# Where the seven-product pairs stand: w_out and gate/up shifted by one pair, and `down` begun with plain steps

## The chip, the cores and the metric

One NeuronCore of a Trainium2 chip runs the kernel. Its engines each work through an instruction queue of their own, in program order, and wait for each other by semaphores: TensorE (PE in the profile, with its weight loads as PEld), VectorE (DVE), ScalarE (ACT), GpSimd (POOL, hardly used here) and SyncE (SP, which issues the DMAs). Matmul results go to PSUM, everything else lies in SBUF. The metric is the device time of one execution in microseconds, the median of several runs.

## What is computed

A decoder block on 256 tokens of width 2048: RMSNorm, two attention branches merged through sigmoid gates, an output projection with a residual, RMSNorm, a SwiGLU feed-forward of width 5632 with a residual, and a last RMSNorm. The change touches what follows the two branches:

```python
mixed = g_a * (y_a @ w_branch_a[l]) + g_b * (y_b @ w_branch_b[l])
h = h + mixed @ w_out[l]                                   # 2048 x 2048
hn = rmsnorm(h, ffn_norm[l])
h = h + (jax.nn.silu(hn @ w_gate[l]) * (hn @ w_up[l])) @ w_down[l]
return rmsnorm(h, final_norm)
```

All inputs and the output are float32.

## The kernel before

**Precision.** [...] A product is made of three matmuls: hi x hi, lo x hi, hi x lo. For weights, ScalarE writes `wh` (L927) and VectorE `wl` (L928).

**Jobs and steps.** The program is a list of jobs. A plain job multiplies one slab of 512 output columns: the 256 tokens are two row tiles t = 0, 1, and each has one PSUM accumulator of 128x512. The reduction goes in groups of four k-tiles (one DMA of 1 MB into a `raw` buffer) and each group in two steps of two k-tiles. So a plain step has 2 x 2 x 3 = 12 matmuls of 512 columns (L1026 for hi x hi and lo x hi, L1031 for hi x lo).

**Pairs with seven products.** Gate and up, and the slabs of `down` two by two, are taken as pairs: slabs a and b share the left operand. With the chunks of 512 along the reduction numbered 0, 1, 2, ..., chunks 0 and 1 of both slabs make a 2 x 2 block product (two token tiles by two chunks, two chunks by two slabs), which is done with seven products instead of eight, P1 to P7. Four accumulators are named by row tile and slab: 11, 21 (slab a) and 12, 22 (slab b). The products need sums of the left operand's blocks (`row_sums`, made once for a left operand by four VectorE adds and a cut) and differences of weights: four subtractions T1 to T4 of VectorE (L843, 128x2048), done in place in the raw buffers. A step of a product has 6 matmuls. The other chunks are plain, in steps written `a20` here: slab a, chunk 2, first k-tile 0. Four results that are needed alone are copied out of PSUM by ScalarE (`alone`, L683).

**Order.** The steps form one list. At step s the program first issues the weight cuts of step s + 3 (`split_until(s + AHEAD)`, with four buffers each for `wh` and `wl`), then whatever was put off to this step by `later` or `at`, then the matmuls of s. Each engine then executes in that order. The weights have 6 raw buffers by this part of the program; a buffer's next load is issued when its last cut has been issued. Everything of 128x1024 elements (left operands, their cuts, sums, results) lies in a pool of 33 slots. PSUM has four banks for accumulators and four for transposes.

**Around the change.** The four w_out slabs wo0 to wo3 are plain jobs with two accumulators each. After each, `wout_done` adds the residual (L643), sums the squares (ScalarE, L166), scales the rows by an estimate of the norm from the first slab (`hr`, L654; its root and `invert`, L155 to L159), and transposes them (`turned`, L207; PE, then ScalarE to `hF`). `cut` makes hi and lo of the transposed chunk (L217, L218). The true norm enters later as `hs`. Then follow the pairs gu0 to gu10 of gate and up, and dn0 and dn1 of `down`; each gate/up pair gives one chunk `aF` of the left operand of `down`. `feed` cuts such a chunk shortly before `down` uses it; `leave` adds the residual to the results of dn0 and multiplies by the last norm's gain. The products stand at the start of every pair, with chunk 2 and 3's steps for slab a between them:

P1, a20, P5, P2, a22, P3, P6, a30, P4, P7, a32, b20, b22, b30, b32, then all other chunks.

Of the kernel before, what the change touches and what calls it, by code (L numbers as in the profile page):

```python
# [24 lines left out]
F32R = mybir.dt.float32r  # L25
# [4 lines left out]
P = 128  # L30
NT = 2
# [37 lines left out]
def block_kernel(ctx: ExitStack, tc, x, positions, attn_norm, w_in, q_norm, w_uq, kv_norm, w_ukv,  # L69
# [72 lines left out]
    L = {}  # L142


    def rstd(ss, n, name):

        v, r, t = [const([P, NT], name + x) for x in ("_v", "", "_t")]

        def root():
            nc.vector.tensor_reduce(out=v, in_=ss, axis=mybir.AxisListType.X, op=OP.add)  # L150
            nc.vector.tensor_scalar(v, v, 1.0 / n, EPS, op0=OP.mult, op1=OP.add)
            nc.scalar.activation(t, v, AF.Sqrt)
# [167 lines left out]
    def pair(w, kt, ops, begin, name):  # L320
        jobs.append(dict(w=w, kt=kt, ops=ops, begin=begin, name=name))

    later_q = {}
    now = [0]
# [291 lines left out]
                nc.vector.tensor_mul(g[:, t], ps[t], g[:, t])  # L616
        return done

    mh, ml = [], []
    hop, hF, aF, aop = {}, {}, {}, {}  # L620
    ssh = const([P, NT, 4], "ssh")
    ssf = const([P, NT, 4], "ssf")
    R["h"], h_root, h_invert = rstd(ssh, D, "rstd_h")
    R["h0"], h0_root, h0_invert = rstd(ssh[:, :, 0:1], 512, "rstd_h0")
    hs = const([P, NT], "hs")

    def wa_done(c):
        def done(ps):
            a, b = gates["a", c], gates["b", c]
            for t in range(NT):  # L630
                nc.vector.tensor_mul(a[:, t], ps[t], a[:, t])
            nc.vector.tensor_add(b, a, b)
            mh.append(big([P, 4, S], f"mh{c}", F32R))
            ml.append(big([P, 4, S], f"ml{c}", F32R))
            spread(2, b, mh[c], ml[c], f"mT{c}")
        return done

    def wout_done(c):

        def done(ps):  # L640
            h = xt[c]
            for t in range(NT):
                nc.vector.tensor_add(h[:, t], ps[t], h[:, t])  # L643
                sumsq(h[:, t], ssh[:, t, c:c + 1])
            d = 4 if c == 0 else 1
            if c == 0:
                later(1, h0_root)
                later(3, h0_invert)
            st = {}

            def rows():
                st["n"] = big([P, NT, 512], f"hr{c}")
                for t in range(NT):
                    nc.scalar.mul(st["n"][:, t], h[:, t], R["h0"][:, t:t + 1])  # L654
                hF[c] = big([P, 4, S], f"hF{c}")

            def ready():
                hop[c] = cut(hF[c], f"h{c}")
                if c == 1:
                    hop["s"], add, finish = row_sums(hF[0], hF[1], "h")  # L660
                    later(1, add)
                    later(2, finish)
            later(d, rows)
            for i in range(2):
                later(d + 1 + i, lambda i=i: turned(st["n"], hF[c], f"hT{c}", 2 * i, "ffn", 4 * c))
            later(d + 3, ready)
            if c == 3:
                later(3, h_root)
                later(5, h_invert)

                def both():
                    v = L["h0_v"]
                    nc.vector.tensor_mul(hs, v, R["h0"])
                    nc.vector.tensor_mul(hs, hs, R["h"])
                later(6, both)
        return done

    def alone(jb, A, B):

# [2 lines left out]
        for u, dst, key in (("P1", A[:, 0], "22"), ("P5", B[:, 1], "12"), ("P6", B[:, 0], "22"), ("P7", A[:, 1], "22")):  # L682
            later(pos[u], lambda dst=dst, key=key: nc.scalar.copy(dst, ps[key]))  # L683

    def gu_begin(c):
        def begin(jb):
            ps, pos = jb["accs"], jb["pos"]
            A, B = big([P, NT, 512], f"ga{c}"), big([P, NT, 512], f"up{c}")
            alone(jb, A, B)

            def gate():
                for t, k in enumerate(("11", "21")):
                    nc.vector.tensor_add(A[:, t], ps[k], A[:, t])
# [24 lines left out]
    def dn_begin(j):  # L718
        def begin(jb):
            ps, pos = jb["accs"], jb["pos"]  # L720
            A, B = big([P, NT, 512], f"dA{j}"), big([P, NT, 512], f"dB{j}")
            alone(jb, A, B)
            for i, x in enumerate((A, B)):
                later(pos["P7"] + 3 + i, lambda i=i, x=x: nc.vector.tensor_add(xt[2 * j + i], xt[2 * j + i], x))
# [75 lines left out]
        gate_job("a", c)  # L800
    for c in range(4):
        job(w_branch_a[:, 512 * c:512 * (c + 1)], 8, ylhs("a"), wa_done(c), f"wa{c}")
    for c in range(4):
        job(w_out[:, 512 * c:512 * (c + 1)], 16, lhs_of(mh, ml), wout_done(c), f"wo{c}")
    for c in range(11):
        pair((w_gate[:, 512 * c:512 * (c + 1)], w_up[:, 512 * c:512 * (c + 1)]), 16, hop, gu_begin(c), f"gu{c}")
    for j in range(2):
        pair([w_down[:, 512 * c:512 * (c + 1)] for c in (2 * j, 2 * j + 1)], 44, aop, dn_begin(j), f"dn{j}")


    groups, steps = [], []
# [20 lines left out]
    def pair_steps(jb):  # L832


        ops, n = jb["ops"], jb["kt"] // 4
        wa, wb = jb["w"]
        G = {}

        def get(*cs):
            for x, c in cs:  # L840
                G[x, c] = add_group((wa, wb)[x], 4 * c, 4)

        sub = lambda o, x, y: (lambda: nc.vector.tensor_sub(raws[G[o]], raws[G[x]], raws[G[y]]))  # L843
        get((0, 0), (1, 0), (0, 2), (0, 1), (1, 1), (0, 3), (1, 2), (1, 3), *[(x, c) for c in range(4, n) for x in range(2)])

        def seven(name, key, src, lhs, pre=None):
            for k0 in (0, 2):
                add_step(jb, G[src], k0, [(key, lhs(k0))], pre if k0 == 0 else None, name)
# [7 lines left out]
        seven("P1", "22", (0, 0), A(0, 0), sub((1, 0), (1, 0), (0, 0)))  # L856
        eight(0, 2, 0)
        seven("P5", "12", (1, 0), S_(1))
        seven("P2", "11", (0, 1), A(1, 0), sub((1, 0), (1, 1), (1, 0)))
        eight(0, 2, 2)  # L860
        seven("P3", "12", (1, 1), S_(4), sub((0, 0), (1, 0), (0, 0)))
        seven("P6", "22", (1, 0), S_(2), sub((0, 1), (0, 1), (1, 0)))
        eight(0, 3, 0)
        seven("P4", "21", (0, 1), A(1, 1))
        seven("P7", "22", (0, 0), S_(3))
        eight(0, 3, 2, "a")
        for c in (2, 3):
            for k0 in (0, 2):
                eight(1, c, k0, "b")
        for c in range(4, n):  # L870
# [132 lines left out]
    for s, st in enumerate(steps):  # L1003
# [64 lines left out]
```

## Time and profile before

| what | value |
|---|---|
| median of 3 runs (lowest, highest) | 1347.22 us (1346.87, 1348.03) |
| profiled execution, its own time | 1348.63 us |
| span of its instructions | 1346.8 us |
| PE busy, DVE busy, ACT busy | 1305.4, 993.2, 782.8 us |
| mean granted TensorE clock | 0.943 |

The span runs from the first to the last instruction of the program; the execution's own time is 1.8 us more. A busy PE is one with a matmul in it. Idle time of an engine matters where another engine that sets the end has to wait for it. [...]

### The profile page before, as it was taken

What the parts mean: (1) busy time and instruction counts of PE and PEld (TensorE: products, weight loads), DVE (VectorE), ACT (ScalarE), POOL (GpSimd) and SP (SyncE); (2) the same over time, 40 slices, a digit from 0 to 9 for tenths busy, and PEclk for the clock granted to TensorE, in tenths of its full rate; (3) what the DMA queues carried; (4) which work ended last, traced back from release to release, by engine and by line L of the source; (5) the groups of instructions that cost most, each with busy time, mean ns of one, the idle gap of its engine ahead of it and who ended that gap; (6) DMA issues with size and microseconds to landing.
All of it is one profiled execution on the core that took longest, in us unless ns stands there. A gap on an engine that the chain in (4) does not pass through costs nothing.

```text
span 1346.8 us, 15873 instructions
## 1 busy us (share of the span) xinstructions
PE 1305.4 (97%) x5990; PEld 1081.8 (80%) x5990; DVE 993.2 (74%) x1212; ACT 782.8 (58%) x1000; POOL 2.1 (0%) x11
## 2 busy tenths in 40 slices
PE   8999999999999999998999999999999989998997
PEld 6888888888888888776887878778787868886885
DVE  5766667674565565578888998889888997579654
ACT  6455555654444454656666666667666665446553
POOL 0000000000000000000000000000000000000000
PEclk9999999999999999999999999999999989998998
DMA  8565544455555565543557545674457637553731
GB/s 295 187 205 182 164 159 153 160 174 189 187 183 160 190 244 188 188 157 118 173 209 250 191 151 185 223 249 156 159 186 249 220 124 250 190 185 108 267 125 63
DMA packets 126969, 249.06 MB, mean 185 GB/s; under 512 B 4486, under 2 KB 9132, under 8 KB 126892
## 3 DMA queue, kind: packets, MB, share of 16 engines
q1 hardware_dynamic: 126620, 247.78, 54.8%
q8 instruction: 47, 0.77, 0.2%
q10 hardware_dynamic: 272, 0.26, 0.1%
q14 instruction: 30, 0.25, 0.1%
HBM read 245.93 MB, written 2.10 MB: 184 GB/s over the span
## 4 chain that ended last, share of the span: by engine, by line
PE 92%; DVE 5%; ACT 2%; issue 1%; DMA 0%; ACTq 0%; SPq 0%; DVEq 0%
PE acc L1026 58%; PE acc L1031 29%; DVE wl L928 2%; DVE raw L843 1%; PE aT_tp L207 1%; ACT wh L927 1%; PE sb L435 1%; ACT junk L166 1%; PE ya L471 0%; PE yb L471 0%; DMA x<-in_x_dram 0%; PE sa L435 0%; PE hT_tp L207 0%; PE xT_tp L183 0%; ACT hr L654 0%
## 5 line engine op out<-in xcount | busy, mean ns | idle before, releaser
L928 DVE TENSOR_TENSOR wl<-raw,wh 128x1024 fp32r<-128x1024 f32 (+2 forms) x546 | 649.2, 1211 | 289.7 <-ACT wh L927 265.8
L927 ACT CAST wh<-raw 128x1024 fp32r<-128x1024 f32 (+2 forms) x546 | 568.1, 1044 | 406.0 <-PE acc L1026 359.6
L1026 PE MATMUL acc<-wh,xh 128*128 128x512 f32 (+1 forms) x512 | 139.4, 394 | 0.0
L1026 PE MATMUL acc<-wh,xl 128*128 128x512 f32 (+1 forms) x512 | 135.5, 387 | 0.0
L1031 PE MATMUL acc<-wl,xh 128*128 128x512 f32 (+1 forms) x512 | 135.3, 386 | 0.0
L843 DVE TENSOR_TENSOR raw<-raw,raw 128x2048 f32<-128x2048 f32 x52 | 118.8, 2285 | 0.4
L1026 PEld LDWEIGHTS acc<-wh,xl 128*128 128x128 f32 x512 | 95.7, 189 | 19.7
L1031 PEld LDWEIGHTS acc<-wl,xh 128*128 128x128 f32 x512 | 95.7, 189 | 19.3
L1026 PEld LDWEIGHTS acc<-wh,xh 128*128 128x128 f32 x512 | 92.0, 190 | 15.2
L1026 PE MATMUL acc<-wh,h2h 128*128 128x512 f32 x176 | 47.1, 390 | 0.0
L1031 PE MATMUL acc<-wl,h2h 128*128 128x512 f32 x176 | 47.1, 389 | 0.0
L1026 PE MATMUL acc<-wh,h3h 128*128 128x512 f32 x176 | 47.1, 389 | 0.0
L1026 PE MATMUL acc<-wh,h2l 128*128 128x512 f32 x176 | 47.0, 389 | 0.0
L1026 PE MATMUL acc<-wh,h3l 128*128 128x512 f32 x176 | 47.0, 389 | 0.0
L1031 PE MATMUL acc<-wl,h3h 128*128 128x512 f32 x176 | 47.0, 389 | 0.0
L1026 PEld LDWEIGHTS acc<-wh,h3h 128*128 128x128 f32 x176 | 33.0, 188 | 6.9
L1031 PEld LDWEIGHTS acc<-wl,h2h 128*128 128x128 f32 x176 | 33.0, 188 | 6.9
L1026 PEld LDWEIGHTS acc<-wh,h3l 128*128 128x128 f32 x176 | 33.0, 188 | 6.9
L1026 PEld LDWEIGHTS acc<-wh,h2l 128*128 128x128 f32 x176 | 33.0, 188 | 6.9
L1031 PEld LDWEIGHTS acc<-wl,h3h 128*128 128x128 f32 x176 | 33.0, 188 | 6.9
L1026 PEld LDWEIGHTS acc<-wh,h2h 128*128 128x128 f32 x176 | 33.0, 188 | 6.8
L1031 PE MATMUL acc<-wl,hq0h 128*128 128x512 f32 x88 | 28.5, 405 | 9.4 <-DVE wl L928 9.4
(444 smaller groups left out, 2013.8 us busy)
## 6 DMA issues: line engine op xcount, KB each, us to landing
raw<-in_w_in_dram SPq DMA_DIRECT2D x59, 1024.0 KB, 5.1
raw<-in_w_gate_dram SPq DMA_DIRECT2D x44, 1024.0 KB, 6.9
raw<-in_w_up_dram SPq DMA_DIRECT2D x44, 1024.0 KB, 5.3
raw<-in_w_down_dram SPq DMA_DIRECT2D x44, 1024.0 KB, 5.2
raw<-in_w_out_dram SPq DMA_DIRECT2D x16, 1024.0 KB, 5.1
raw<-in_w_branch_b_dram SPq DMA_DIRECT2D x8, 1024.0 KB, 5.1
raw<-in_w_branch_a_dram SPq DMA_DIRECT2D x8, 1024.0 KB, 6.0
raw<-in_w_uq_dram SPq DMA_DIRECT2D x4, 768.0 KB, 4.5
```

The costliest lines, as they stand in the source:

```text
L166: nc.scalar.activation(junk[:, :src.shape[-1]], src, AF.Square, accum_out=acc)
L207: nc.tensor.transpose(tp[:, k, t * P:(t + 1) * P], nat[:, t, (j + k) * P:(j + k + 1) * P], ident)
L435: nc.tensor.matmul(ps[:, t, :], lhsT=l, rhs=r, start=i == 0, stop=i == len(mm) - 1)
L843: sub = lambda o, x, y: (lambda: nc.vector.tensor_sub(raws[G[o]], raws[G[x]], raws[G[y]]))
L927: nc.scalar.copy(hi, v)
L928: nc.vector.tensor_sub(lo, v, f32(hi))
L1026: nc.tensor.matmul(accs[key], lhsT=lhs(k)[i], rhs=hi[:, k], start=i == 0 and k == 0 and jb["first"][key] == s, stop=False, skip_group_chec ...
L1031: nc.tensor.matmul(accs[key], lhsT=lhs(k)[0], rhs=lo[:, k], start=False, stop=(st["read"] or jb["last"][key] == s) and k == 1, skip_group_ ...
```

## The change

The four w_out slabs become two pairs. The first pair (wo0) is computed plainly, the second (wo1) with the seven products on chunks 0 and 1. The first gate/up pair, gu0, is computed plainly, the others as before. In `down` the products move to chunks 3 and 4 (`region`), behind six plain steps of slab a; chunks 3 and 4 and the row sums are cut once and kept for both `down` pairs. The gated sum of the branches is now transposed to `mF` and cut afterwards. The work that follows w_out and the feeds of `down` are put off by other numbers of steps; the root on ScalarE comes a step after its sum (`apart`); the gain's multiplication in dn0 is one operation, three steps later.

```diff
+PLAIN = "a00 b00 a02 b02 a10 b10 a12 b12 a20 b20 a22 b22 a30 a32 b30 b32"
+BETWEEN = "1 a20 5 2 a22 3 6 a30 4 7 a32 b20 b22 b30 b32"
+DOWN = "a00 a02 a10 a12 a20 a22 1 a50 5 2 a52 3 6 a60 4 7 a62 b00 b02 b10 b12 b20 b22 b50 b52 b60 b62"
...
+            if apart:
+                later(1, lambda: nc.scalar.activation(t, v, AF.Sqrt))
...
-            spread(2, b, mh[c], ml[c], f"mT{c}")
+            mF[c] = big([P, 4, S], f"mF{c}")
+            for i in range(2):
+                later(2 + i, lambda i=i: turned(b, mF[c], f"mT{c}", 2 * i))
+            def ready():
+                mop[c] = cut(mF[c], f"m{c}")
+                if c == 1:
+                    at("wo0", 6, sums)
+            def sums():
+                mop["s"], add, finish = row_sums(mF[0], mF[1], "m")
+                add()
+                later(2, finish)
+            later(4, ready)
...
-    def wout_done(c):
...
+    def h_leaves(c, ps, keys):
+        h = xt[c]
+        for t in range(NT):
+            nc.vector.tensor_add(h[:, t], ps[keys[t]], h[:, t])
+            sumsq(h[:, t], ssh[:, t, c:c + 1])
+        d, e = ((6, 3), (4, 2), (2, 2), (3, 2))[c]
+        if c == 0:
+            later(2, h0_root)
+            later(5, h0_invert)
...
+        later(d, rows)
+        for i in range(2):
+            later(d + e + i, lambda i=i: turned(st["n"], hF[c], f"hT{c}", 2 * i, "ffn", 4 * c))
+        later(d + e + 2, ready)
+        if c == 3:
+            later(1, h_root)
+            later(4, h_invert)
...
+    def wout_begin(j):
+        def begin(jb):
+            ps, pos = jb["accs"], jb["pos"]
+            to_residual(jb, j, "wo")
+            later(pos["a"] + 1, lambda: h_leaves(2 * j, ps, ("11", "21")))
+            later(pos["b"], lambda: h_leaves(2 * j + 1, ps, ("12", "22")))
+        return begin
...
                 for t, k in enumerate(("11", "21")):
-                    nc.vector.tensor_add(A[:, t], ps[k], A[:, t])
-                    nc.scalar.activation(A[:, t], A[:, t], AF.Silu, scale=hs[:, t:t + 1])
+                    if seven:
+                        nc.vector.tensor_add(A[:, t], ps[k], A[:, t])
+                    nc.scalar.activation(A[:, t], A[:, t] if seven else ps[k], AF.Silu, scale=hs[:, t:t + 1])
...
-                    nc.vector.tensor_mul(h[:, t], h[:, t], L["gf"][j][:, i])
+                later(3, lambda: nc.vector.tensor_mul(h, h, L["gf"][j][:, i, None, :].to_broadcast([P, NT, 512])))
...
-    for c in range(4):
-        job(w_out[:, 512 * c:512 * (c + 1)], 16, lhs_of(mh, ml), wout_done(c), f"wo{c}")
+    for j in range(2):
+        pair(slabs(w_out, j), 16, mop, wout_begin(j), f"wo{j}", (None, (0, 1))[j], (PLAIN, BETWEEN)[j])
     for c in range(11):
...
+             (0, 1) if c else None, BETWEEN if c else PLAIN)
     for j in range(2):
...
+        pair(slabs(w_down, j), 44, aop, dn_begin(j), f"dn{j}", (3, 4), DOWN)
...
     for j in range(2):
-        at(f"dn{j}", -6, feed(j, 0))
-        at(f"dn{j}", -5, feed_sums(j))
-        at(f"dn{j}", -2, feed(j, 2))
-        at(f"dn{j}", -1, feed(j, 1))
-        at(f"dn{j}", 8, feed(j, 3))
-        for c in range(4, 11):
-            at(f"dn{j}", 22 + 4 * (c - 4) - 4, feed(j, c))
-    at("dn0", 0, load_gfin)
+        at(f"dn{j}", -4, feed(j, 0))
+        at(f"dn{j}", -2, feed(j, 1))
+        at(f"dn{j}", 1, feed(j, 2))
+        at(f"dn{j}", 6, feed(j, 5))
+        at(f"dn{j}", 13, feed(j, 6))
+        for c in range(7, 11):
+            at(f"dn{j}", 34 + 4 * (c - 7) - 4, feed(j, c))
+    for i in range(2):
+        at("dn0", i, feed(0, 3 + i))
+    at("dn0", 2, feed_sums)
+    at("dn0", 30, load_gfin)
```

In `pair_steps` the order of steps and of weight loads now follows the string: a digit stands for the two steps of that product, `a20` for one plain step; chunks beyond it are plain and follow. `to_residual` holds what `dn_begin` did with `alone` and the two adds (L724), now one step after P7 instead of three. `pos["a"]` and `pos["b"]` are the step behind the last one of slab a and b.

## Rows read from the trace of the kernel before

**Rows 1.** The page, parts 1 and 6: busy times; loads of `down`, median us to landing.

```profile
PE 1305.4 (97%) x5990; PEld 1081.8 (80%) x5990; DVE 993.2 (74%) x1212; ACT 782.8 (58%) x1000; POOL 2.1 (0%) x11
...
raw<-in_w_down_dram SPq DMA_DIRECT2D x44, 1024.0 KB, 5.2
```

**Rows 2.** Waits of PE, whole span: total us, times, longest us.

```profile
PE acc L1031 <- DVE wl L928: 12.3, 14, 1.7
PE hT_tp L207 <- ACT hr L654: 4.3, 6, 2.0
PE acc L1026 <- DVE up L700: 4.2, 1, 4.2
...
PE acc L1026 <- DVE x L729: 3.6, 1, 3.6
PE acc L1026 <- ACT wh L927: 1.7, 2, 0.9
```

**Rows 3.** Stretches: length, busy us (instructions) of each engine, PEclk, DMA share, GB/s.

```profile
1088.35:1092.53 4.18, 0.00 (x2) 0.00 (x1) 4.15 (x6) 3.50 (x5) 0.00 (x0) 0.83 0.00 0
1091.44:1098.27 6.83, 5.74 (x16) 4.57 (x17) 6.73 (x8) 1.46 (x2) 0.00 (x0) 0.50 0.00 0
...
1217.73:1224.56 6.83, 6.11 (x14) 4.79 (x15) 4.85 (x7) 4.65 (x8) 0.00 (x0) 0.50 0.00 0
608.39:610.66 2.27, 0.23 (x3) 0.01 (x1) 0.65 (x1) 2.27 (x5) 0.00 (x0) 0.95 0.00 0
```

**Rows 4.** Groups of instructions by form: busy us, mean ns | idle before, releasers.

```profile
L928 DVE TENSOR_TENSOR wl<-raw,wh 128x1024 fp32r<-128x1024 f32 x530 | 635.1, 1221 | 275.1 <-ACT wh L927 257.5 <-PE acc L1026 8.5 <-PE sb L435 1.5
L843 DVE TENSOR_TENSOR raw<-raw,raw 128x2048 f32<-128x2048 f32 x52 | 118.8, 2285 | 0.4
...
L643 DVE TENSOR_TENSOR x<-acc,x 128x512 f32<-128x512 f32 x8 | 5.2, 686 | 3.4 <-PE acc L1031 3.4
...
L927 ACT CAST wh<-raw 128x1024 fp32r<-128x1024 f32 x530 | 555.6, 1052 | 390.8 <-PE acc L1026 344.4 <-DVE raw L843 17.5 <-issue 16.4
```

**Rows 5.** Timeline, end of slab wo1: start us, us, instruction [idle before <-releaser].

```profile
556.09 1.07 PE L1026 MATMUL acc<-wh,mh 128*128 128x512 f32 x4
...
556.47 1.23 DVE L928 TENSOR_TENSOR wl<-raw,wh 128x1024 fp32r<-128x1024 f32 x1 [0.32 <-ACT wh L927]
...
558.55 1.29 DVE L643 TENSOR_TENSOR x<-acc,x 128x512 f32<-128x512 f32 x2 [0.86 <-PE acc L1031]
...
559.28 0.63 ACT L166 ACTIVATE junk<-x 128x512 bf16<-128x512 f32 x1 [2.84 <-DVE x L643]
...
560.66 1.03 ACT L927 CAST wh<-raw 128x1024 fp32r<-128x1024 f32 x1
561.60 1.33 ACT L654 ACTIVATE hr<-x,rstd_h 128x512 f32<-128x512 f32 x2
...
562.37 0.33 PE L207 MATMUL hT_tp<-ident,hr 128*128 128x128 f32 x1 [0.68 <-ACT hr L654]
```

**Rows 6.** Timeline, gu0: first and last of the five operations of `invert`.

```profile
622.25 0.16 DVE L155 RECIPROCAL rstd_h<-rstd_h_t 128x2 f32<-128x2 f32 x1
...
623.04 0.16 DVE L159 TENSOR_TENSOR rstd_h<-rstd_h,rstd_h_t 128x2 f32<-128x2 f32 x1
```

**Rows 7.** Timeline, a gate/up pair from a22 to P6's wait.

```profile
709.72 1.07 PE L1026 MATMUL acc<-wh,h2h 128*128 128x512 f32 x4
...
712.44 0.62 PE L1026 MATMUL acc<-wh,hq1h 128*128 128x512 f32 x2
...
715.74 6.89 DVE L928 TENSOR_TENSOR wl<-raw,wh 128x1024 fp32r<-128x1024 f32 x6
...
717.00 0.73 PE L1031 MATMUL acc<-wl,hq0h 128*128 128x512 f32 x2 [0.78 <-DVE wl L928]
```

**Rows 8.** Timeline, start of dn0: P1, and a20 at its second accumulator.

```profile
1083.29 0.62 PE L1026 MATMUL acc<-wh,d_0h 128*128 128x512 f32 x2
...
1092.53 1.65 PE L1026 MATMUL acc<-wh,d_2h 128*128 128x512 f32 x3 [4.18 <-DVE up L700]
```

More of the change, by code (lines that the diff above doesn't have):

```diff
@@ L142, in block_kernel, with rstd @@
     L = {}
-    def rstd(ss, n, name):
+    def rstd(ss, n, name, apart=False):
         v, r, t = [const([P, NT], name + x) for x in ("_v", "", "_t")]
@@ L318, in job, with pair @@
         jobs.append(dict(w=w, kt=kt, n=w.shape[1], lhs=lhs, done=done, name=name))
-    def pair(w, kt, ops, begin, name):
-        jobs.append(dict(w=w, kt=kt, ops=ops, begin=begin, name=name))
+    def pair(w, kt, ops, begin, name, region, order):
+        jobs.append(dict(w=w, kt=kt, ops=ops, begin=begin, name=name, region=region, order=order))
     later_q = {}
@@ L617, in wb_done @@
         return done
-    mh, ml = [], []
+    mF, mop = {}, {}
     hop, hF, aF, aop = {}, {}, {}, {}
@@ L632, in done @@
             nc.vector.tensor_add(b, a, b)
-            mh.append(big([P, 4, S], f"mh{c}", F32R))
-            ml.append(big([P, 4, S], f"ml{c}", F32R))
-            spread(2, b, mh[c], ml[c], f"mT{c}")
-        return done
-    def wout_done(c):
-        def done(ps):
-            h = xt[c]
-            for t in range(NT):
[L643 to L666, printed above, removed]
-            if c == 3:
[L668 to L676, printed above, removed]
@@ new lines, in done, with rows, ready, both @@
+            mF[c] = big([P, 4, S], f"mF{c}")
[10 more added lines that the diff above has]
+            later(4, ready)
+        return done
+    def h_leaves(c, ps, keys):
[7 more added lines that the diff above has]
+            later(5, h0_invert)
+        st = {}
+        def rows():
+            st["n"] = big([P, NT, 512], f"hr{c}")
+            for t in range(NT):
+                nc.scalar.mul(st["n"][:, t], h[:, t], R["h0"][:, t:t + 1])
+            hF[c] = big([P, 4, S], f"hF{c}")
+        def ready():
+            hop[c] = cut(hF[c], f"h{c}")
+            if c == 3:
+                hop["s"], add, finish = row_sums(hF[0], hF[1], "h")
+                later(2, add)
+                later(4, finish)
+        later(d, rows)
[5 more added lines that the diff above has]
+            later(4, h_invert)
+            def both():
+                nc.vector.tensor_mul(hs, L["h0_v"], R["h0"])
+                nc.vector.tensor_mul(hs, hs, R["h"])
+            later(5, both)
@@ L683, in alone, with to_residual @@
             later(pos[u], lambda dst=dst, key=key: nc.scalar.copy(dst, ps[key]))
+    def to_residual(jb, j, name):
+        if jb["region"] is None:
+            return
+        A, B = big([P, NT, 512], f"{name}A{j}"), big([P, NT, 512], f"{name}B{j}")
+        alone(jb, A, B)
+        for i, x in enumerate((A, B)):
+            later(jb["pos"]["P7"] + 1 + i, lambda i=i, x=x: nc.vector.tensor_add(xt[2 * j + i], xt[2 * j + i], x))
+    def wout_begin(j):
[5 more added lines that the diff above has]
+        return begin
     def gu_begin(c):
@@ L720, in begin @@
             ps, pos = jb["accs"], jb["pos"]
[L721 to L724, printed above, removed]
+            to_residual(jb, j, "dn")
             def leave(i):
@@ L835, in pair_steps, with get, seven @@
         ops, n = jb["ops"], jb["kt"] // 4
-        wa, wb = jb["w"]
+        order = jb["order"].split()
+        seven_of = jb["region"]
+        r0, r1 = seven_of or (0, 0)
+        done = max([r1] + [int(u[1]) for u in order if u[0] in "ab"]) + 1
         G = {}
-        def get(*cs):
-            for x, c in cs:
-                G[x, c] = add_group((wa, wb)[x], 4 * c, 4)
+        def get(x, c):
+            if (x, c) not in G:
+                G[x, c] = add_group(jb["w"][x], 4 * c, 4)
+        for u in order:
+            for x, c in {"1": ((0, r0), (1, r0)), "2": ((0, r1), (1, r1))}.get(u, (("ab".find(u[0]), int(u[-2:-1] or 0)),)):
+                if x >= 0:
+                    get(x, c)
+        for c in range(done, n):
+            get(0, c)
+            get(1, c)
         sub = lambda o, x, y: (lambda: nc.vector.tensor_sub(raws[G[o]], raws[G[x]], raws[G[y]]))
[L844 to L848, printed above, removed]
+        def seven(name, key, src, lhs, *pre):
+            for k0, before in zip((0, 2), (*pre, None, None)):
+                add_step(jb, G[src], k0, [(key, lhs(k0))], before, name)
         def eight(x, c, k0, tag=None):
@@ L855, in pair_steps @@
         S_ = lambda i: (lambda k0: row_sum(ops, i - 1, k0))
[L856 to L870, printed above, removed]
+        T1, T2 = sub((1, r0), (1, r0), (0, r0)), sub((1, r0), (1, r1), (1, r0))
+        T3, T4 = sub((0, r0), (1, r0), (0, r0)), sub((0, r1), (0, r1), (1, r0))
+        products = {"1": ("22", (0, r0), A(r0, 0), T1), "5": ("12", (1, r0), S_(1)), "2": ("11", (0, r1), A(r1, 0), T2),
+                    "3": ("12", (1, r1), S_(4), T3), "6": ("22", (1, r0), S_(2), T4), "4": ("21", (0, r1), A(r1, 1)),
+                    "7": ("22", (0, r0), S_(3))}
+        for u in order:
+            if u in products:
+                seven("P" + u, *products[u])
+            else:
+                eight("ab".index(u[0]), int(u[1]), int(u[2]), u[0])
+        for c in range(done, n):
             for x, k0 in ((0, 0), (0, 2), (1, 0), (1, 2)) if c == n - 1 else ((0, 0), (1, 0), (0, 2), (1, 2)):
                 eight(x, c, k0, "ab"[x])
+        jb["pos"]["a"] = max(jb["pos"].get(u, 0) for u in ("a", "P2", "P4", "P7"))
     for jb in jobs:
```

33 lines of the change are left out of this document (18 added, 15 removed).

## The prediction

> **What bounds the kernel now.** First the busy line of the page [rows 1]: TensorE (PE) is busy 97% of 1346.8 us, VectorE (DVE) 74%, ScalarE (ACT) 58%. So the time is PE's instructions plus PE's waits, and the change keeps the number of both kinds of matmul (below). I read PE's waits next [rows 2]: after the start there are 24 of them, 26.1 us of idle in all (12.3 for `wl`, 4.3 for the rows of h, 4.2 and 3.6 for an accumulator at the start of each `down` pair, 1.7 for `wh`). Each costs more than its idle: two matmuls take 0.62 us and four 1.07 [rows 7], so one starts 0.225 after the other, a row is 0.39 long, and 0.16 of it normally lies under the next one; and the first pair after a wait takes 0.73 us [rows 7] instead of 0.62. That is 0.27 per wait, 6.5 for 24, so 32.6 us.
>
> Nine of them are one repeated wait. In each gate/up pair the chain T3, lo, lo, T4, lo of DVE runs without a gap, and the lo of P6 comes 0.78 us late, 1.05 with the 0.27 [rows 7]. gu2 to gu10 keep exactly this order, so 9.5 us stay. 23.1 remain: two in the third and fourth slab of w_out, in gu0 and gu1, and in both `down` pairs.
>
> Then the clock [rows 3]. [...] PE was busy 5.74 and 6.11 us of these; at 0.95 that work takes 0.5/0.95 as long, so 2.7 and 2.9 us were lost. After an idle of 2.0 us in gu0 it stayed at 0.95. So before loses 23.1 + 5.6 = 28.7 us in places that the change rewrites. This is the most it can win.
>
> **The change, part by part.** *Matmuls.* A plain step has 12 and lasts 2.72 us (from h2h to hq1h) [rows 7]; a step of a product has half, 1.36. w_out goes from 384 matmuls to 192 + 180, gu0 from 180 to 192, `down` keeps its number: 0 us. The 52 T subtractions (2.29 us) also stay 52 [rows 4]: wo1 gains four and gu0 loses four. One set of row sums goes to w_out and one leaves dn1.
>
> *The w_out slabs of before* leave in a burst: two adds, two sums of squares on ACT, the next wh, then hr, and the transposes are already queued on PE [rows 5]. Now rows and transposes are two or three steps apart, and those of the last two slabs fall into plain gu0, where a step gives DVE 2.72 us for a 1.15 us lo. I cost gu0 at nothing: that idle DVE time is the cover; without it the products' waits in gu0 (1.15 and 1.68 idle) would be back.
>
> *wo0 to wo1, the new place.* h0's scale must now be ready inside the products of wo1. Clock t=0 at P1's first matmul; ACT and DVE work in program order, with lookahead of three steps. Durations: lo 1.15 pitch [rows 7], wh 1.05, T 2.29 [rows 4], add 0.65, two sums of squares 1.4 from the first add's start plus 0.73 [rows 5], inverse 0.97 [rows 6]. In a plain stretch a lo starts 0.38 after its step (556.09 and 556.47) [rows 5]; so lo(a20), issued in the last plain step (from -2.72), is done at -1.1. Then:
> - DVE adds 11, 21: -1.1 to 0.2. ACT squares until 1.0, wh(P5) to 2.0, DVE lo(P5) to 3.3.
> - DVE adds 12, 22 only now: 3.3 to 4.6. a20's accumulator 21 takes the bank of the old 12 (a bank is handed on in the order of last use: dn0's second accumulator waited for `up`, which reads 12 [rows 8]). PE wants it at 2.95 and gets it 0.74 after the add's start, 4.0: **1.05 lost.**
> - ACT squares to 5.4, wh(P5b) 6.4, lo 7.6, the root's two small operations 8.0, T2 10.3, lo(P2a) 11.4. PE needs that at 10.1: **1.3 lost**; P2a ends at 11.9.
> - DVE lo, lo, inverse: 14.7; ACT's hr starts, and the transposes follow 0.77 behind it [rows 5], at 15.5; the second half of hr 0.65 later. PE stood ready at 11.9: **4.0 lost**. During this DVE catches up, so the usual wait at P6 is gone.
>
> Sum 6.35. Behind the transposes stand all of PE's matmuls, nothing else waits for them: the cut operands are used from gu0 on. The idle stretch is 3.6 us, nearest to the 3.6 and 4.18 that were followed by the half clock, so I add 2.6 for about 5.5 busy us at 0.50; the ends are 0 and 2.9.
>
> *gu0 to gu1.* ACT now reads gate from PSUM at the end of a plain pair: two Silu and two scalings hold up wh until 0.4, lo ends at 2.7, the mul that frees 12 delays a20 by 0.45, and P6 by 0.4 (two adds fewer). 0.85 instead of 1.05.
>
> *dn0.* Six plain steps (16.3 us and 0.7 of transposes) now run ahead of P1, so the accumulator wait and both others go. But DVE gets more in there: two cuts before, then from about -1 without a gap: cut of chunk 1, two lo, cut 3, `up` (4 x 0.65), lo, cuts 2 and 4, lo, four row-sum adds (4 x 0.63), T1, two lo, two row-sum lo, two lo, cut 5: 15 operations of 1.15 + 2.6 + 2.5 + 2.3 = 24.6 us, ending at 23.6. a50, two steps behind P1, starts at 19.7 and needs the low half of chunk 5 at 20.6: **3.0 lost**. Afterwards T2 to T4 and the cut of chunk 6 make P6's two steps late by 1.3 and 0.9. Sum 5.2; idle 2.9 us lies between the 2.0 that left the clock alone and the 3.6; I take no drop, ends 0 and 2.8.
>
> *dn1* has no row sums, no cuts 3 and 4, no `up`, and the gain products are put three steps later: DVE needs 14 of 16.3 us before P1, and chunk 5 is cut at 18.7 for 19.9. Only P6b is late: 0.9.
>
> After: 6.35 + 2.6 + 0.85 + 5.2 + 0.9 = 15.9. Gain 28.7 - 15.9 = 12.8.
>
> By rows, the half clock is a matter of what the idle stretch was like [rows 3]. [...]
>
> **The rivals.**
> 1. *No half clock in wo1.* For it: an idle of 2.0 left it alone; against: 3.6 did not. 28.7 - 13.3 = 15.4 won, 1331.8.
> 2. *The wait for hr is much shorter*, if DVE and ACT run closer together than my chain has it (it adds twelve durations): without the 4.0 and the clock 19.4 won, 1327.8. Against: every link is a first-in queue in rows 5.
> 3. *Both new idle stretches halve the clock*, or dn0's cut 5 is later by two lo: 28.7 - 18.7 = 10 or a little less, 1337 to 1340.
> 4. *Slower: weights late in `down`.* P1 to P7 hold four of six weight buffers for 17 steps, and five b chunks have to follow through the rest. A load takes 5.2 us to land [rows 1], two plain steps take 5.44. If loads did not overlap at all, each of the ten in dn0 and dn1 could cost up to 5.2; from 28.7 - 15.9 = 12.8 us on, three loads unhidden, it is slower: with four, 1355. Against: gate/up holds four buffers in the same way and rows 2 name no weight DMA.
> [...]
>
> **How the numbers follow.** The profiled execution took 1348.63 us (span 1346.8, 1.8 around it); 12.8 less is 1335.8. The runs' median 1347.22 lies 1.4 below it, so I predict 1334.4. Chances: forecast 0.43, rival 1 0.27, rival 2 0.10, rival 3 0.12, rival 5 0.03, rival 4 0.03, and 0.02 that all of it cancels to nothing. Range: from 1329 (between rivals 1 and 2, since the 4.0 may be half) to 1340. About 0.2% (2.7 us) is what a measurement of this kernel tells from no change: faster 0.94, same 0.03, slower 0.03.
>
> **What would show it.** Right: no PE wait for `x`, `up` or `wh` at the start of dn0 and dn1; hT waits of gu0 gone, one of 3 to 4 us in wo1 between the inverse and hr; a wait near 3 us at a50 of dn0 for the low half of chunk 5; the wait at P6 of gu2 to gu10 still 0.78. Wrong: PE idle over 5 us in wo1, more than one stretch at 0.50 ahead of dn0, or a PE, ACT or DVE wait for weight DMA. The forecast fails most easily in the order of operations around wo1's P2, where one more thing ahead of the inverse moves everything behind it.

## The result, and the profile after

The changed kernel took 1336.36 us (median of four runs, 1335.32 to 1336.74), the kernel before 1347.62 beside it (1346.87 to 1348.21). The ratio is 0.9915, 95% interval 0.9898 to 0.9933: faster by 11.3 us. Forecast were 1334.4 and a range of 1329 to 1340. The profiled execution took 1336.74 us, with a span of 1335.0. Of the versions below, e7, e11 and e12 had one execution each of 2963 to 7503 us, in e7 the profiled one; these are left out, so e7's trace is not read.

The busy line of the page, changed kernel; it answers to the first row of [rows 1]:

```profile
PE 1301.5 (97%) x5990; PEld 1079.8 (81%) x5990; DVE 989.6 (74%) x1202; ACT 784.1 (59%) x1002; POOL 2.1 (0%) x11
```

PE has the same 5990 matmuls and is busy 3.9 us less. 2.8 of it is work that no longer runs at half clock (5.74 and 6.11 busy us at 0.50 [rows 3], now 6.28: half of the difference). The rest of the gain must be waits. PE's waits in the changed kernel (total us, times, longest us), the two rows of the start left out, against [rows 2]:

```profile
PE acc L1074 <- DVE wl L970: 10.4, 14, 1.0
...
PE hT_tp L213 <- ACT hr L670: 3.2, 1, 3.2
PE acc L1069 <- DVE d_5l L224: 2.2, 1, 2.2
...
PE acc L1069 <- DVE ga L737: 1.2, 1, 1.2
PE acc L1069 <- DVE x L659: 0.8, 1, 0.8
```

17.8 us in 18 waits, where before had 26.1 in 24. The waits for `up` and `x` at the start of dn0 and dn1 and those for `wh` are gone, and the six for `hr` have become one of 3.2. What each place loses now, read from the starts of PE's steps against their undisturbed 1.36 and 2.72 us, next to the forecast:

| place | before | forecast | measured after |
|---|---|---|---|
| w_out and gu0 (wo1 after the change) | 9.0 | 8.95 | 8.8 |
| gu1 | 1.05 | 0.85 | 1.46 |
| dn0 | 9.05 | 5.2 | 4.5 |
| dn1 | 9.8 | 0.9 | 1.8 |
| sum | 28.9 | 15.9 | 16.6 |

So the half of the change that concerns w_out and gate wins nothing (10.0 before, 10.3 after), and `down` wins all of it (18.8 before, 6.3 after).

The timeline of the changed kernel inside wo1 (start us, us, instruction, idle before and its releaser):

```profile
562.03 0.96 PE L1069 MATMUL acc<-wh,m2h 128*128 128x512 f32 x3 [0.75 <-DVE x L659]
...
565.92 2.29 DVE L890 TENSOR_TENSOR raw<-raw,raw 128x2048 f32<-128x2048 f32 x1
565.93 1.28 ACT L156 ACT_TABLE_LOAD   x1
...
567.34 1.98 ACT L969 CAST wh<-raw 128x1024 fp32r<-128x1024 f32 x2
...
568.12 3.49 DVE L970 TENSOR_TENSOR wl<-raw,wh 128x1024 fp32r<-128x1024 f32 x3
569.40 0.73 PE L1074 MATMUL acc<-wl,m1h 128*128 128x512 f32 x2 [0.95 <-DVE wl L970]
571.53 0.16 DVE L161 RECIPROCAL rstd_h<-rstd_h_t 128x2 f32<-128x2 f32 x1
...
572.51 1.34 ACT L670 ACTIVATE hr<-x,rstd_h 128x512 f32<-128x512 f32 x2 [3.20 <-DVE rstd_h L165]
573.29 1.52 PE L213 MATMUL hT_tp<-ident,hr 128*128 128x128 f32 x4 [3.16 <-ACT hr L670]
```

All three forecast waits are there, in their order: a20's accumulator (0.75 idle, 1.05 lost), the low half of P2a behind T2 (0.95 idle, 1.24 lost), and the transposes behind the inverse. (The high half of an operand, `hi`, is its cast to fp32r, L969 for weights; the low half, `lo`, is the operand less that, L970.) The reader is to see the queue: T2 (565.92), then three low halves (568.12), and only then the reciprocal (571.53), though the root it needs was written at 567.4. What no step of the forecast had is the table load on ScalarE (565.93, 1.28 us), which the root brings with it. It costs nothing here: it lies beside T2, and VectorE has no gap from T2 to the reciprocal.

Then the clock, in four stretches of the changed kernel: the wait for `hr` and the 6.83 us behind it, the wait at a50 of dn0 and the 6.83 us behind that (length; busy us of PE, PEld, DVE, ACT, POOL; PEclk, the granted clock, a share of full speed as the profile reads it; DMA share; GB/s):

```profile
570.13:573.29 3.16, 0.00 (x2) 0.00 (x1) 3.02 (x8) 0.78 (x2) 0.00 (x0) 0.94 0.26 17
572.88:579.71 6.83, 6.28 (x18) 4.94 (x19) 5.27 (x4) 6.83 (x12) 0.00 (x0) 0.50 0.40 148
1104.97:1107.19 2.22, 0.00 (x1) 0.00 (x1) 2.22 (x3) 0.21 (x1) 0.00 (x0) 1.00 0.00 0
1107.19:1114.02 6.83, 6.83 (x30) 5.67 (x31) 6.80 (x6) 4.52 (x5) 0.00 (x0) 1.00 0.01 2
```

After 3.16 us without a matmul the clock stood at 0.50 for 6.83 us, and PE was busy 6.28 of them. Two matmuls start 0.85 us after the two before them there (575.46 to 576.31), and 0.45 at 1.00 (1109.14 to 1109.59), so about half of the 6.28 is lost, 3.1. After the 2.22 at a50 it stayed at 1.00. The wait at a50 has the forecast cause; VectorE works without a gap ahead of it:

```profile
1103.64 2.36 DVE L970 TENSOR_TENSOR wl<-raw,wh 128x1024 fp32r<-128x1024 f32 x2
...
1105.91 1.22 DVE L224 TENSOR_TENSOR d_5l<-aF,d_5h 128x1024 fp32r<-128x1024 f32 x1
...
1107.19 1.20 PE L1069 MATMUL acc<-wh,d_5l 128*128 128x512 f32 x4 [2.22 <-DVE d_5l L224]
```

gu1 is the place that came out dearer. The timeline of its start, changed kernel:

```profile
652.86 1.28 ACT L729 ACT_TABLE_LOAD   x1
...
654.15 1.27 ACT L729 ACTIVATE ga<-acc,hs 128x512 f32<-128x512 f32 x2
...
656.53 2.93 ACT L969 CAST wh<-raw 128x1024 fp32r<-128x1024 f32 x3
...
658.75 1.28 DVE L737 TENSOR_TENSOR ga<-acc,ga 128x512 f32<-128x512 f32 x2
...
659.48 0.96 PE L1069 MATMUL acc<-wh,h2h 128*128 128x512 f32 x3 [1.17 <-DVE ga L737]
```

gu0's gate now ends the pair, so the load of the Silu table stands right ahead of it, and the two Silu, two scalings, the next high half, VectorE's low half and its `mul` follow 1.28 us later.

### The profile page after: what moved, and what is told of

It reads as the page before. It is cut to its first block, busy times and chain, and to the rows that moved or that the text cites. A ratio compares the mean times of both kernels' runs of the same rounds, so it can differ in the third digit from the quotient of the medians.

```text
span 1335.0 us, 15875 instructions
## 1 busy us (share of the span) xinstructions
PE 1301.5 (97%) x5990; PEld 1079.8 (81%) x5990; DVE 989.6 (74%) x1202; ACT 784.1 (59%) x1002; POOL 2.1 (0%) x11
## 4 chain that ended last, share of the span: by engine, by line
PE 93%; DVE 4%; ACT 1%; issue 1%; DMA 0%; ACTq 0%; SPq 0%; DVEq 0%
PE acc L1069 59%; PE acc L1074 30%; DVE wl L970 2%; DVE raw L890 1%; PE aT_tp L213 1%; PE sb L441 1%; PE ya L477 0%; PE yb L477 0%; DMA x<-in_x_dram 0%; ACT junk L172 0%; PE sa L441 0%; PE hT_tp L213 0%; ACT wh L969 0%; PE xT_tp L189 0%; PE mT_tp L213 0%
## 5 line engine op out<-in xcount | busy, mean ns | idle before, releaser
L970 DVE TENSOR_TENSOR wl<-raw,wh 128x1024 fp32r<-128x1024 f32 (+2 forms) x546 | 649.6, 1212 | 293.0 <-ACT wh L969 270.0
L969 ACT CAST wh<-raw 128x1024 fp32r<-128x1024 f32 (+2 forms) x546 | 567.9, 1044 | 405.8 <-PE acc L1069 362.7
```

Source lines behind the costliest of these rows:

```text
L969: nc.scalar.copy(hi, v)
L970: nc.vector.tensor_sub(lo, v, f32(hi))
```

## The experiments

Two theories stood at the start: that all of the gain comes from `down`, the stalls of w_out being only exchanged for others; and that each half wins a part. Then: that each stall left has its own cause in the order of the queues, against that ScalarE and VectorE are short of time there, so that a stall removed comes back at the next step. The versions were measured on several chips, on which the kernel before read 1347.5 to 1349.1, so what a difference of 1 or 2 us from the changed kernel's 1336.36 is due to is read from the trace.

**The two halves alone.** e1_down_only keeps the old w_out jobs and seven products in gu0 (first diff, against the changed kernel); e2_wout_only keeps the old order of `down` (second).

```diff
-    for j in range(2):
-        pair(slabs(w_out, j), 16, mop, wout_begin(j), f"wo{j}", (None, (0, 1))[j], (PLAIN, BETWEEN)[j])
+    for c in range(4):
+        job(w_out[:, 512 * c:512 * (c + 1)], 16, lhs_of(mh, ml), wout_done(c), f"wo{c}")
```

```diff
-        pair(slabs(w_down, j), 44, aop, dn_begin(j), f"dn{j}", (3, 4), DOWN)
+        pair(slabs(w_down, j), 44, aop, dn_begin(j), f"dn{j}", (0, 1), BETWEEN)
```

> Only the part of the change that concerns the down projection is made (products on chunks 3 and 4 behind six plain steps, row sums once); the four w_out slabs and gu0 stand as in the kernel before. Theory A, the two halves are independent and the down half is the whole gain: before, dn0 and dn1 lost 9.0 and 9.8 us to waits and half clock, after 4.5 and 1.8, so 12.5 us less than before, near 1335, a ratio of 0.991. Theory B, the shift of the products in w_out and gate/up carries at least half of the gain: 1341 or more.

> Only the w_out and gu0 part is made; the down pairs stand as in the kernel before. Theory A: the waits taken from the w_out slabs, gu0 and gu1 (10.0 us) come back as the waits and the half clock in wo1 and the wait at the start of gu1 (8.8 and 1.5 us), so no change: 1347 to 1348, within 1.5 us of before. Theory B: 1342 or less.

Measured: 1336.73 for `down` alone (ratio to before 0.9914, 0.9901 to 0.9928), 1347.6 for w_out alone (0.9997, 0.9988 to 1.0006). The first equals the whole change, the second the kernel before: the first theory in both. Which part of the `down` half brings how much (the six plain steps, the cuts and sums made once, the later multiplication) was not separated. In e2 the half clock comes three times, once in wo1 and at the start of both `down` pairs: the w_out half removes waits of its own stretch and pays the same back in one long one.

e1 showed something else. The wait at a50 is 2.23 idle there, as in the changed kernel, but here the clock fell behind it (windows, e1_down_only):

```profile
1107.30:1110.70 3.40, 3.40 (x10) 2.63 (x9) 3.37 (x3) 1.05 (x1) 0.00 (x0) 0.50 0.02 5
```

And yet e1 is no slower: P6's two waits of dn0 (0.78 and 0.60 idle in the changed kernel) are 0.22 and under 0.2 here. While PE ran at half clock VectorE caught up. The 1.7 us lost behind a50 (half of 3.40) are given back as 1.4 at P6.

**The wait for `hr` in wo1.** Transposes of slab 1 one step later (e3), or rows and transposes of both slabs four steps later (e4).

```diff
-        d, e = ((6, 3), (4, 2), (2, 2), (3, 2))[c]
+        d, e = ((6, 3), (4, 3), (2, 2), (3, 2))[c]       # e3_one_step
+        d, e = ((10, 4), (8, 3), (2, 2), (3, 2))[c]      # e4_rows_later
```

> The changed kernel with one number altered: the transposes of the second w_out chunk come three steps after its rows instead of two, so that one more product step of 1.36 us stands ahead of them. Theory A, the half clock in wo1 belongs to the length of that one idle stretch: the idle falls from 3.2 to about 1.8 us, the clock stays full, and 1.4 + 2.7 us go: near 1332.3. Theory B, the half clock comes from the three waits of wo1 together or from the time in the program: it stays, and only 1.4 us go: near 1335.

> The changed kernel with the rows and transposes of the first two w_out chunks four steps later and further apart (rows 10 and 8 steps after the add, transposes 4 and 3 behind them), so that PE never stands in wo1 for the scaled rows. Theory A: the wait of 3.2 us and the half clock of 6.8 us go, the two smaller waits of wo1 stay, and the wait at P6, which VectorE had caught up during the long one, comes back with about 1 us: 3.4 + 2.7 - 1 = 5 us less, near 1331. Theory B, VectorE and not the order of the transposes is what bounds wo1: the wait turns up at the products instead and 1335 or more is measured.

Measured: 1333.29 (0.9889, 0.9876 to 0.9903) and 1332.76 (0.9886, 0.9873 to 0.9900), each a little above its expectation. In e3 the wait is 1.78 idle and the clock in wo1 stays whole, as the first theory had it; that is 1.4 and 3.1 won, of which a second wait for `hr` (0.29 idle, 0.56 with its 0.27) takes some back: w_out and gu0 together are 3.8 shorter. In e4 the wait is gone, but P3 and P6 of wo1 now wait 0.70 and 1.45 for their low halves. In both the 3.41 us at 0.50 stand behind a50, and dn0 is no more than 0.2 longer for it, as in e1. The one long wait had been giving VectorE time.

**The repeated wait at P6.** T4 is moved from ahead of P6 to ahead of P4, its only user. The raw buffer that it reads is then let go later.

```diff
-        ... "6": ("22", (1, r0), S_(2), T4), "4": ("21", (0, r1), A(r1, 1)),
+        ... "6": ("22", (1, r0), S_(2)), "4": ("21", (0, r1), A(r1, 1), T4),
...
+                if u == "4":
+                    steps[-2]["also"] = G[1, r0]
```

> The changed kernel with T4 issued before P4, which is the product that reads it, instead of before P6, in every pair with seven products; the weight buffer that T4 reads is kept until then. Theory A, the repeated wait at P6 comes from the place of T4 in VectorE's queue (2.3 us ahead of P6's lo), not from VectorE's total work: nine waits of 1.05 us in gu2 to gu10 go, and most of the 3.8 us of P6 waits in dn0 and dn1: 9 to 13 us less than the changed kernel, 1323 to 1327. Theory B, VectorE's total work through the products is the bound: the wait moves to P4 or P7, at most 3 us are won, 1333 or more.

Measured: 1328.44 (0.9852, 0.9839 to 0.9866), 7.9 less than the changed kernel, somewhat short of the expectation. The waits at P6 are gone from all of gu2 to gu10. One pair now follows the next after 42.1 us instead of 42.8. The wait of 1.05 is traded for about a third of it at P4, which now stands behind T4. gu2 to gu10 give 6.5 of the 7.9. dn0 and dn1 win only 0.4 and 0.6, where most of 3.8 was expected: half clock follows a50 here, and in dn1 a wait of 0.59 for a high half stands in P6's place. The waits of e5_t4_late have two for `wl` left, of 14:

```profile
PE acc L1078 <- DVE wl L973: 1.2, 2, 1.0
```

**Cutting chunks 3 and 4 of `down` earlier** (their cuts at three and one steps ahead of dn0, for 0 and 1).

```diff
-        at("dn0", i, feed(0, 3 + i))
+        at("dn0", 2 * i - 3, feed(0, 3 + i))
```

> The changed kernel with the cuts of chunks 3 and 4 for dn0 issued 3 and 1 steps before dn0 instead of at its first and second step, so that VectorE does 2.3 us of the queue ahead of chunk 5's cut before dn0 begins. Theory A, that queue is what a50 of dn0 waits for: its wait of 2.2 us idle falls to 0.3 or less, 2 us less than the changed kernel, near 1334.3. Theory B, ScalarE's casts at the end of gu10, which have less idle time than VectorE there, become late instead and PE waits at the start of dn0: 1336 or more.

Measured: 1336.18 (0.9909, 0.9896 to 0.9923), the wait at a50 still 2.21. The first theory fell. The timeline of e6 at the end of gu10 shows why the earlier place bought nothing:

```profile
1076.76 1.22 DVE L224 TENSOR_TENSOR d_3l<-aF,d_3h 128x1024 fp32r<-128x1024 f32 x1
1077.89 1.28 DVE L728 TENSOR_TENSOR ga<-acc,ga 128x512 f32<-128x512 f32 x2
...
1078.61 1.34 ACT L729 ACTIVATE ga<-ga,hs 128x512 f32<-128x512 f32 x2 [2.08 <-DVE ga L728]
...
1079.85 1.32 ACT L731 ACTIVATE ga<-ga,hs 128x512 f32<-128x512 f32 x2
...
1081.08 1.03 ACT L969 CAST wh<-raw 128x1024 fp32r<-128x1024 f32 x1
...
1082.14 1.23 DVE L970 TENSOR_TENSOR wl<-raw,wh 128x1024 fp32r<-128x1024 f32 x1 [2.97 <-ACT wh L969]
```

VectorE stands idle 2.97 us for a high half that ScalarE makes only after gate's two Silu and two scalings. Its gapless run up to a50 begins behind that idle. Chunk 3's low half (1076.76) has left the run, but it now stands ahead of the add (1077.89) that gate's Silu waits for, so the run begins 1.25 us ahead of dn0 and no longer 2.39: the 1.1 taken out of the run is lost at its start. Chunk 4's stays inside the run.

**The Silu table early:** a Silu of one column (a value that nothing reads) in gu0's step 6, with VectorE and PE busy and nothing waiting for ScalarE.

```diff
+    at("gu0", 6, lambda: nc.scalar.activation(warm, warm, AF.Silu))
```

> The changed kernel with one Silu of a single column on ScalarE at the seventh step of gu0, so that the table load of 1.28 us that stands ahead of gu0's gate (and behind the root's) happens in the middle of gu0. Theory A, this load is what the sum of the prediction missed at gu1 (1.46 us lost instead of the 0.45 at a20): 1.0 us less, near 1335.3. Theory B, ScalarE is late there for the two Silu and two scalings themselves: no change, 1336.4.

Measured: 1333.79 (0.9896, 0.9881 to 0.9911; three executions, 1333.45 to 1335.66), 2.6 less than the changed kernel. The two intervals overlap, so the cause is taken from the later versions that hold this line. Timeline of e12_sum:

```profile
626.37 1.28 ACT L1049 ACT_TABLE_LOAD   x1
...
651.23 1.26 ACT L729 ACTIVATE ga<-acc,hs 128x512 f32<-128x512 f32 x2
...
656.43 1.11 PE L1074 MATMUL acc<-wh,h2h 128*128 128x512 f32 x4
```

The load stands in the middle of gu0, and a20 of gu1 (656.43) waits for nothing. gu1 takes 41.8 us, against 43.2 in e5, which differs there only by the load: 1.4, the whole wait. So theory A holds, with a little more than its 1.0.

**All four together** (e4, e5, e6, e7).

> The changed kernel with the four alterations together: rows and transposes of the first two w_out chunks later, T4 behind P6, cuts 3 and 4 of dn0 early, the Silu table loaded early. Theory A, each wait has its own cause and they add: from 1332.8 (the run with the rows later, where a half clock of 3.4 us after a50 also cost 1.6) 9.5 at gu2 to gu10, 2.1 at P6 of wo1, 3.8 at P6 of dn0 and dn1, 2.5 + 1.6 at a50 and 1.0 at gu1, so 20 less: near 1312. Theory B, they share VectorE's time: 1320 or more.

Measured: 1324.64 (0.9824, 0.9810 to 0.9837). This is the fastest version found, 11.7 us below the changed kernel and 23 below before, but some 12 above what the first theory expected. Measured alone, the four edits bring 3.6, 7.9, 0.2 and 2.6; together 11.7 of these 14.3. Theory B. Two rows of PE's waits of e8_all say where it stays:

```profile
PE acc L1074 <- DVE d_5l L224: 2.2, 1, 2.2
...
PE acc L1074 <- ACT woA L697: 1.8, 1, 1.8
```

The second is new: in wo1 an accumulator waits for ScalarE's copy of a result, which now stands behind the late rows, the transposes' outputs and the cuts.

**What the inverse stands behind.** T2 later, with T3 ahead of P3. The edit moved it in every pair, not only in that of w_out, which the expectation left out.

```diff
-        ... "2": ("11", (0, r1), A(r1, 0), T2),
-                    "3": ("12", (1, r1), S_(4), T3),
+        ... "2": ("11", (0, r1), A(r1, 0)),
+                    "3": ("12", (1, r1), S_(4), lambda: (T2(), T3())),
```

> The changed kernel with the pre-sum T2 of the seven-product pair of w_out (2.29 us of VectorE) issued with T3 ahead of P3 and no longer ahead of P2. Theory A: T2 stands ahead of both the low half for P2a and the inverse of the row scale, so it sets both waits of that pair: the 0.95 idle (1.24 lost) at P2a goes, and the transposes' wait for hr falls from 3.16 idle to 2.1 to 2.6, with the half clock perhaps gone too: near 1331.5, or 1334 if the clock still drops. Theory B: the pair is bound by what VectorE and ScalarE have to do in all, so the waits only move to P3 and P6: 1335 or more. The changed kernel stands at 1336.4.

Measured: 1341.85 (0.9957, 0.9945 to 0.9970), 5.5 slower than the changed kernel. Theory A fell for the wait for `hr`. P2a's wait is gone, so PE is ready 1.2 earlier, but the other wait is 3.50 instead of 3.16: the transposes start 14.26 us behind P1's start and no longer 15.12, so the later T2 brought them only 0.9 nearer. Timeline of e9_t2_late in wo1:

```profile
564.39 1.28 ACT L156 ACT_TABLE_LOAD   x1
...
565.80 1.98 ACT L969 CAST wh<-raw 128x1024 fp32r<-128x1024 f32 x2
...
566.87 2.36 DVE L970 TENSOR_TENSOR wl<-raw,wh 128x1024 fp32r<-128x1024 f32 x2 [1.23 <-ACT wh L969]
569.14 0.16 DVE L161 RECIPROCAL rstd_h<-rstd_h_t 128x2 f32<-128x2 f32 x1
...
570.90 1.51 PE L213 MATMUL hT_tp<-ident,hr 128*128 128x128 f32 x4 [3.50 <-ACT hr L670]
```

With T2 out of the way VectorE is idle 1.23, and the reciprocal still stands behind two low halves. These wait for two high halves, which stand behind the table load and the root: without T2 ScalarE's chain sets the time, and it ends only 0.9 earlier. In the other pairs T2 and T3 now run one after the other, and P6 waits 1.18 instead of 0.78 (716.55, for one): 3.7 in gu2 to gu10, 1.46 in gu1 and 1.96 in `down`, less 1.34 in w_out and gu0, make 5.7, against 5.5 measured.

**Chunk 5 of `down` cut earlier**, at step 3 of dn0.

```diff
-        later(2, finish)
+        later(4, finish)
...
-        at(f"dn{j}", 6, feed(j, 5))
+        at(f"dn{j}", 6 if j else 3, feed(j, 5))
```

> The changed kernel with chunk 5 of down's activations fed at step 3 of the first pair and no longer at step 6, and the row sums finished two steps later. Theory A: its low half at a50 was merely late in the order, and VectorE has room ahead of it: the 2.22 idle at a50 falls to 0.3 or less, with some of it coming back (1.5 lost) at P2a, where T-sums and low halves now queue: near 1335. Theory B: VectorE's total up to P2a binds, whatever the order: 1336.4, as the changed kernel. If half clock follows a wait here that it did not follow there, 1.6 more.

Measured: 1335.08 (0.9908, 0.9894 to 0.9921), not clear of the changed kernel. The time is that of theory A, the cause is not. The wait at a50 is gone, but P2a waits 1.37 and P6 1.42 and 0.61: 3.4 of idle in dn0, where it was 3.6. VectorE's total binds there, as theory B has it. The 1.3 came from wo1 for the most part, where the same 3.16 us of wait was followed by only half as long a stretch at 0.50 (windows, e10_chunk5_early):

```profile
572.60:576.00 3.40, 3.00 (x9) 2.33 (x10) 2.87 (x2) 3.40 (x7) 0.00 (x0) 0.50 0.77 296
```

**Every subtraction as late as its user allows**: T2 ahead of P3, T3 ahead of P6's second half, T4 ahead of P4, with e7, e10 and the rows of w_out later.

```diff
+        d, e = ((6, 5), (4, 4), (2, 2), (3, 2))[c]
...
+                    "3": ("12", (1, r1), S_(4), T2), "6": ("22", (1, r0), S_(2), None, T3),
```

> The changed kernel with all pre-sums as late as their products allow (T2 ahead of P3, T3 ahead of P6's second half, T4 ahead of P4 in every seven-product pair), the Silu table loaded early with a Silu of one column, chunk 5 fed at step 3, and w_out's row scale and transposes one to two steps later. Theory A: each wait left has its own cause in the order: from the 1328.4 of the kernel with T4 late, w_out gives 6 to 7 (8.8 lost there to 1.5 to 3), gate 1.0, down 2 to 3: 1317 to 1319. Theory B: ScalarE and VectorE are short of time in w_out as such, so most of what goes in one place comes back in the next, as in the kernel with all four alterations (1324.6): 1323 or more.

Measured: 1330.64 (0.9872, 0.9854 to 0.9890): slower than T4 late alone. Theory B holds for w_out: it wins 0.4 over e5 instead of 6 to 7, since wo1 waits 2.07 and 0.92 for ScalarE's copies of results and 0.61 for a high half. dn0 waits 1.87 for a low half. What makes it slower than e5 lies elsewhere: gu2 to gu10, with T2 and T3 late as well, take 2.3 us longer, dn1 1.0.

**One step more for the inverse:** e5, e3's step, e7 and e10, and the inverse one step earlier in VectorE's queue.

```diff
-            later(5, h0_invert)
+            later(4, h0_invert)
```

> The kernel with T4 late (1328.4) with four more edits: the transposes of w_out's second slab one step later (3.1 less when done alone), the Silu of one column in gate's plain pair (1.6 less), chunk 5 fed at step 3 with the row sums finished two steps later (1.3 less), and, new, the five small operations that invert the row scale one step earlier in VectorE's queue, so that they stand behind two low halves and no longer behind three. Theory A: the wait for hr is set by that place in the queue: with one step of transposes and one low half it falls from 3.16 idle to about 0.6 (1.8 by the step alone, 1.15 for the low half), the clock stays whole in w_out, and each edit brings its own: 1321 to 1323. Theory B: the inverse then waits for the square root on ScalarE, which stands behind a table load, so the wait stays near 1.8, and the edits give back some of each other's gain, as in the kernel with four alterations: 1324.6 or more.

Measured: 1326.33 (0.9838, 0.9826 to 0.9851). Timeline of e12_sum in wo1:

```profile
571.48 0.33 PE L213 MATMUL hT_tp<-ident,hr 128*128 128x128 f32 x1 [0.65 <-ACT hr L670]
...
582.37 1.23 DVE L224 TENSOR_TENSOR h1l<-hF,h1h 128x1024 fp32r<-128x1024 f32 x1 [0.45 <-ACT h1h L223]
...
583.51 2.29 DVE L890 TENSOR_TENSOR raw<-raw,raw 128x2048 f32<-128x2048 f32 x1
...
585.89 1.04 ACT L972 CAST wh<-raw 128x1024 fp32r<-128x1024 f32 x1 [3.55 <-DVE raw L890]
...
586.99 0.74 PE L1074 MATMUL acc<-wh,m1h 128*128 128x512 f32 x2 [2.02 <-ACT wh L972]
```

The wait for `hr` is 0.65, as theory A said: it was the place of the reciprocal in VectorE's queue. But PE, now ahead, meets the next chain at P4: rows transposed, cut on ScalarE, cut on VectorE, T4, the high half. 2.02 of idle, and 3.41 us at 0.50 behind it, take back most of what was won (w_out and gu0 are 0.8 shorter than in e5); in e5 the same chain was hidden under the earlier stall.

## Why the prediction was right, point by point

- *The matmuls cost nothing either way*: right; the count is the same and every undisturbed step is 2.72 or 1.36.
- *wo1 loses 6.35 plus 2.6 for the clock*: right in places and cause. 1.05 and 1.24 were forecast as 1.05 and 1.3; the inverse ended 14.3 us behind P1's start, forecast 14.7. That the sum fits so well (8.8 for 8.95) is in part luck: the wait for `hr` cost 3.4 with its 0.27 and not 4.0, the clock 3.1 and not 2.6, and the two errors cancel. The cause of the long wait was named as T2 and the low halves ahead of the inverse; e12 confirms it for the low half. e9 shows that T2's place is worth only 0.9 of its 2.29, since ScalarE's table load and root, which the forecast left out, make a second chain that ends nearly as late.
- *gu0 at nothing*: right.
- *gu1 0.85*: the term was mis-sized, 1.46. The forecast let the Silu run at once; the load of its table (1.28 us) came with it, and e7 and e12 show that this sets the wait. In before this load (647.24, 1.28 us) stood inside gu0, where nothing waited: the Silu started 1.21 us after its end, behind VectorE's add. In the changed kernel the Silu starts at 654.15, 0.01 us after the load's end.
- *dn0 5.2*: 4.5, the same three waits in the same places (2.52 at a50 for 3.0, 1.07 and 0.90 at P6 for 1.3 and 0.9). That the clock stays whole there was luck: it was a choice between the idles of 2.0 and 3.6 in the kernel before, and of the eight traces with this wait of 2.2 us six have half clock behind it (below).
- *dn1 0.9*: mis-sized, 1.8. Only P6's second half was forecast late; its first is late by 0.85 as well.
- *What before loses*: 28.9 for 28.7. Its two drops, 6.83 us at 0.50 each behind the idles of 4.18 and 3.63, were priced at a clock of 0.95; since 0.95 and 1.00 are the same speed (below), half of the busy time is nearer, 2.9 and 3.1 instead of 2.7 and 2.9.
- *gu2 to gu10 keep their wait*: right, 0.74 to 0.79.
- The rivals: the clock did fall in wo1 and not in dn0, as in the forecast. The 13.3 and 18.7 that the rivals start from are the 15.9 less wo1's 2.6 for the clock, and plus dn0's 2.8. No run shows that 2.8: the changed kernel lost nothing to the clock in dn0, e1 1.7. No load of weights was late. For rival 5, more drops of the clock, no run shows a cause: in the changed kernel it read 1.00 in every stretch from 579.71 to 1280 us.

Of the 2.0 between 1334.4 and 1336.36 some 0.7 are in these places (15.9 forecast, 16.6 measured). 1.0 comes from the last step: the forecast took off 1.4, by which the profiled execution of before lay above its median, and that of the changed kernel lies only 0.4 above its own. The other 0.3 is ahead of the change: w_out begins at 513.66 instead of 513.34. The time of one execution scatters by as much as all this (1335.32 to 1336.74).

That w_out gives nothing was in the sum (9.8 left of 10.0) but not said. What stays open is why one wait is followed by half clock and the like one is not.

## What to carry to other kernels

When PE waits for engines with queues in program order, find what the late instruction stands behind in its own queue before moving what seems large: here moving the 2.3 us subtraction brought the transposes only 0.9, because another engine's chain ended nearly as late, and a place behind one low half of 1.15 us was worth 1.1. A long stall also hides the next ones, since it gives the other engines time: its removal brings less than its length wherever they have no slack, which edits tried one by one don't show: 7.9, 3.1, 2.6 and 1.3 alone were 10.0 together, with one more edit. A function that needs another table on ScalarE belongs where nobody waits for ScalarE: the load took 1.28 us here, and moved into the middle of gu0 it was worth 1.4 in gu1.

## What the runs showed of the chip that was not expected

*Two readings of one speed.* Before read 0.95 in undisturbed stretches [rows 3] and 0.943 in the mean, the changed kernel 1.00 and 0.995, at the same 1.07 us for four matmuls. Other executions of the kernel before read 0.991 to 0.993 with the same times. So the step between 0.95 and 1.00 is nothing that the change did.

*The clock behind a wait.* Of the waits of PE after the start, by their idle time:

| idle us | where | followed by |
|---|---|---|
| 1.76, 1.78, 1.87 | e8, e3 (wo1), e11 (dn0) | full clock |
| 2.02, 2.07 | e12, e11 (wo1) | 3.41 us at 0.50 |
| 2.04, 2.05 | gu0 in before and e1 | no drop |
| 2.21 to 2.23 | a50 in e1, e3, e4, e5, e6, e8 | 3.41 us at 0.50 |
| 2.21, 2.22 | a50 in e9 and the changed kernel | full clock |
| 3.16 | wo1 in e10 | 3.41 us at 0.50 |
| 3.15 to 3.50 | wo1 in the changed kernel, e2, e5, e6, e9 | 6.83 us at 0.50 |
| 3.63, 4.18 | starts of dn1 and dn0 in before and e2 | 6.83 us at 0.50 |

The same wait at the same instruction had different consequences, and 2.02 was followed by a drop where 2.05 was not, so the length of the idle alone does not decide. Nor does the stretch at 0.50 begin with the wait or its end: in wo1 of e5 it begins at 571.19, while PE waits from 569.66 to 572.81, in e12 at 588.69, 1.7 us behind the wait's end. In the changed kernel it begins at 572.88, 0.41 ahead of the wait's end. What sets its beginning no run here shows.
